# Order of the first loads and of the first projections in a four-layer transformer kernel on one Trainium2 core

## The chip, the cores and the metric

The program runs on 1 core of one Trainium2 chip. The metric is the device time of one execution in microseconds. The kernel before took 2897.74 us (median of 3 runs, 2897.18 to 2898.78). TensorE is PE below (its weight loads PEld), VectorE DVE, ScalarE ACT, GpSimd POOL, SyncE SP; a "q" behind a name (SPq) is that engine's sequencer, which also issues DMAs.

## What is computed

Two blocks of two layers each over a 512 x 1024 activation, all in float32. Each layer norms its input, projects it, mixes tokens by several kinds of attention, and runs a gated feed-forward part with a short convolution. Only the start of the first layer matters here: the norm, and the first of six column groups of its input projection.

```python
def rmsnorm(x, g):
    xf = x.astype(jnp.float32)
    y = xf * lax.rsqrt(jnp.mean(xf * xf, axis=-1, keepdims=True) + EPS)
    return (y * g.astype(jnp.float32)).astype(x.dtype)
...
def even_mixer(h, w_in, lam_params, subln_g, w_out, rel_table, lam_init):
    B, S, _ = h.shape
    qa, ka, va, qd, kd, vd = split_cols(h @ w_in, EVEN_IN_SPLIT)
```

## The kernel before

The 512 tokens are four tiles of 128 (x0 to x3, t = 0 to 3). Every float32 product is made of three products of split operands: an operand is rounded to a short float (`hi`, on ACT), and the rest is `lo = src - hi` (on DVE); `mm3` (L356 to L360) adds sl*mh, sh*ml and sh*mh into one bank. So a projection matmul needs the split activation (`hh`, `hl`, written by `split`, L390 to L393) and the split weights (`wh`, `wl`).

**Weights** come through `Stream`. `load` (L282) brings the next chunk of 512 KB into one of three raw buffers `wr` by SP's queue; `prep` (L290) makes `wh` on ACT (L300) and `wl` on DVE (L301) and loads further chunks as raw buffers come free. Four split pairs are held.

**The norm** (`pre_norm`, L410) has three stages for a tile: `sumsq` (L420: square with a running sum on ACT), `scale` (L425: `rstd` by two POOL instructions, L405 and L406, then x * rstd * gain row on DVE, L427) and `turn` (L429: eight 128 x 128 transposes on PE, L434, four to a bank, each bank split into hh and hl, half 0 holding column blocks 0 to 3 and half 1 blocks 4 to 7). The gain row is loaded to all partitions (L415). `staged` (L451) writes the stages out skewed over the tiles, and calls `fill` for finished tiles only once all four tiles are in the pipeline.

**The first projection** is "va" in `Block1.even` (L817): four weight chunks c of two column blocks each, 6 matmuls for a chunk and a tile, so 4 x 4 x 6 = 96 matmuls into four banks. `fill(t)` does chunks 0 and 1 for tile t, `vrest` (L891) chunks 2 and 3. Then "vd" and the rest of the layer follow.

**What sets the order.** A tile framework schedules the instructions of each engine itself from the order of the code and the dependencies; on an engine the resulting order is fixed and each instruction waits in turn. Loads at the start go out on SP in the order of the code in `build` (L1857 to L1864): x0, x1, two weight chunks, x2, x3; the gain row and the identity for the transposes go by ACT's queue; three small tables by POOL's.

Of the kernel before, what the change touches and what calls it, by code (L numbers as in the profile page):

```python
# [9 lines left out]
F32 = mybir.dt.float32  # L10
F32R = mybir.dt.float32r
AF = mybir.ActivationFunctionType
# [4 lines left out]
P, S, D, NT, KT = 128, 512, 1024, 4, 8  # L17
# [234 lines left out]
class Blocks:  # L252


    def __init__(self, pool, prefix, n, shape):
        self.pool, self.shape, self.free, self.tag, self.n = pool, shape, deque(f"{prefix}{i}" for i in range(n)), {}, 0
        self.prefix = prefix
# [15 lines left out]
class Stream:  # L273


    def __init__(self, k, w, plan):
        self.k, self.w, self.plan = k, w, plan
        self.loaded = self.prepped = self.lo = self.hi = 0
        self.raw, self.parts = {}, {}
        self.pool = 0  # L280

    def load(self):  # L282
        i = self.loaded
        raw = self.k.sb.tile([P, CH], F32, name=f"wr{i}", tag="wr", bufs=RAW)
        n = self.plan[i][2]
        self.k.nc.sync.dma_start(raw[:, :n], self.w[i, :, :n])
        self.raw[i] = raw
        self.loaded += 1
# [37 lines left out]
class Kernel:  # L326
# [63 lines left out]
    def split(self, hi, lo, src):  # L390

        self.nc.scalar.copy(hi, src)  # L392
        self.nc.vector.tensor_sub(lo, src, hi.bitcast(F32))  # L393
# [16 lines left out]
    def pre_norm(self, gsrc, goff, queue=None):  # L410

        nc = self.nc
        e = self.b8.get()
        grow = e[:, :D]
        (queue or nc.sync).dma_start(grow, self.row(gsrc, goff, D))  # L415
        hb = self.b8.get()
        hs = [hb[:, :D], hb[:, D:]]
        ss = {}

        def sumsq(t):  # L420
            s = self.small()
            nc.scalar.activation(e[:, D:], self.x[t], AF.Square, accum_out=s)
            ss[t] = s

        def scale(t):  # L425
            r = self.rstd(ss.pop(t), 1.0 / D)
            nc.vector.scalar_tensor_tensor(hs[t % 2], self.x[t], r, grow, op0=ALU.mult, op1=ALU.mult)  # L427

        def turn(t):  # L429
            for half in range(2):  # L430
                b = self.bank(2 * t + half)
                for j in range(4):
                    c = (4 * half + j) * P
                    nc.tensor.transpose(b[:, j * P:(j + 1) * P], hs[t % 2][:, c:c + P], self.ident)  # L434
                src = b.rearrange("p (k q) -> p k q", k=4)
                dst = (slice(None), slice(4 * half, 4 * half + 4), slice(t * P, (t + 1) * P))
                self.split(self.hh[dst], self.hl[dst], src)

        def end():
            self.b8.put(e, hb)  # L440

        def first(t):
            sumsq(t)

        def second(t):
            scale(t)

        self.junk = e[:, D:]
        return [first, second, turn], end
# [147 lines left out]
class Job:  # L597
# [15 lines left out]
    def tail(self):  # L613
        return self._tail(self)
# [127 lines left out]
class Block1:  # L742
# [69 lines left out]
        return tail  # L812

    def start(self):
        self.first = self.k.pre_norm(self.k.a["even_norm1"], 0, self.k.nc.scalar)

    def even(self):  # L817
        k, nc, a = self.k, self.k.nc, self.k.a
        stages, end = self.first
        Va, Vd = {}, {}  # L820
        parts, vb = [], {}

        def fill(t):
            if not parts:
                parts.extend(k.ws.get(*[("e", "va", c) for c in range(2)]))
            vb[t] = k.bank(2 * t)
            for c in range(2):
                k.r_tile(vb[t], parts[c], t, (2 * c, 2 * c + 1), S, start=c == 0, stop=c == 3)

        k.staged(stages, fill)  # L830
        end()
        self.vrest("e", "va", 2, vb, Va)
        vb = {t: k.bank(2 * t + 1) for t in range(NT)}
        self.vrest("e", "vd", 0, vb, Vd)
        self.lam()
        self.tables()
        nc.sync.dma_start(k.cols, a["cols"])
        at, n = COLS[2, "bg"]
        nc.vector.tensor_scalar(k.cols[:, at:at + 2 * n], k.cols[:, at:at + 2 * n], 0.5, None, op0=ALU.mult)
        store, out, tabs = {}, {}, {}  # L840

        def begin(p):
            def f(job):
                if p < 4:
                    tabs[p] = [self.table(2 * p), self.table(2 * p + 1)]
                else:
                    tabs[p] = [self.table(4 + p)] * 2
            return f

        def free_qk(p, tail):  # L850
            def f(job):
                fns = tail(job)
                first = fns[0]

                def g():
                    k.blk.put(*store.pop(p))
                    k.blk.put(tabs[p][0])
                    if p < 4:
                        k.blk.put(tabs[p][1])
                    first()  # L860
                    if p == 3:
                        k.blk.put(*Va.values())
                return [g] + fns[1:]
            return f

        def tab(p):
            return lambda hd, t, n: tabs[p][hd][:, 384 - t * P:]

        jobs = []
        for p in range(4):  # L870
            jobs.append(Job(k, Job.PAIR, self.heads64(store, p), tab(p), out, lambda p=p: p in store, begin(p),
                            free_qk(p, self.pair_tail(Va, lambda hd, p=p: (2 * p + hd) * 64, store, p, tabs, out, p))))
        for h in range(4):
            p = 4 + h
            jobs.append(DiffJob(k, self.heads64(store, p), tab(p), out, lambda p=p: p in store, begin(p),
                                free_qk(p, self.diff_tail(Vd, h, out, p))))

        def dense():
            for p in range(8):
                while p - 2 in store:  # L880
                    yield NEED
                yield from self.qk_proj("e", p, store)
            while 3 not in out:
                yield NEED
            yield from self.out_half("e", out)

        k.weave(dense(), k.attention(jobs), 800)
        k.blk.put(*Vd.values())
        return self.out_rest("e", out, 0)
# [9 lines left out]
            V[t] = k.blk.get()  # L899
            k.evac(V[t], vb[t])  # L900

    def lam(self):
        k, nc, a = self.k, self.k.nc, self.k.a
        b = k.blk.get()
        nc.sync.dma_start(b[:, :256], k.row(a["diff_lambda"], 0, 256))
        v = b[:, :256].rearrange("p (a b d) -> p a b d", a=2, b=2)
        pr = b[:, 256:384].rearrange("p (a d) -> p a d", a=2)
        s, e = k.small(2), k.small(2)
        nc.vector.tensor_mul(pr, v[:, :, 0], v[:, :, 1])
        nc.vector.tensor_reduce(s, pr, axis=mybir.AxisListType.X, op=ALU.add)  # L910
        nc.scalar.activation(e, s, AF.Exp)
        nc.vector.tensor_sub(k.neglam, e[:, 1:2], e[:, 0:1])
        nc.vector.tensor_scalar_add(k.neglam, k.neglam, -0.2)
        nc.sync.dma_start(k.subln, k.row(a["diff_subln"], 0, P))
        nc.vector.tensor_scalar(k.subln, k.subln, 0.8, None, op0=ALU.mult)
        k.blk.put(b)
# [928 lines left out]
def build(tc, a, plan):  # L1845
    nc = tc.nc
    with ExitStack() as ctx:
        sb = ctx.enter_context(tc.tile_pool(name="sb", bufs=1))
        ps = ctx.enter_context(tc.tile_pool(name="ps", bufs=1, space=PSUM))
        dram = ctx.enter_context(tc.tile_pool(name="dram", bufs=1, space=DRAM))  # L1850
        k = Kernel(tc, a, plan, sb, ps, dram)
        k.x = [k.const(f"x{t}", [P, D]) for t in range(NT)]
        xin = a["x"][0].rearrange("(t p) d -> t p d", p=P)
        k.ident = k.const("ident_sb", [P, P])
        k.cols = k.const("cols_sb", [P, a["cols"].shape[1]])
        b1 = Block1(k)
        nc.sync.dma_start(k.x[0], xin[0])  # L1857
        b1.start()
        nc.scalar.dma_start(k.ident, a["ident"])
        nc.sync.dma_start(k.x[1], xin[1])  # L1860
        k.ws.load()
        k.ws.load()
        for t in range(2, NT):
            nc.sync.dma_start(k.x[t], xin[t])  # L1864
        k.mhalf = k.const("mhalf", [P, 16])
        nc.gpsimd.memset(k.mhalf, -0.5)
        k.neglam = k.const("neglam", [P, 1])
        k.subln = k.const("subln_sb", [P, P])
        k.hh = k.const("hh", [P, KT, S], F32R)
        k.hl = k.const("hl", [P, KT, S], F32R)  # L1870
        ff = b1.even()
        ff = b1.odd(ff)
        b2 = Block2(k)
        ff = b2.mix(0, ff)
        ff = b2.mix(1, ff)
        b2.end(ff)
# [39 lines left out]
```

## Time and profile before

| | |
|---|---|
| median of the runs | 2897.74 us (2897.18 to 2898.78) |
| the profiled execution | 2899.27 us, of which the span from first to last instruction is 2897.2 us |
| PE busy | 98% of the span, 13612 matmuls |
| DVE, ACT, POOL busy | 54%, 38%, 4% |
| first slice of 40 (72 us) | PE busy 7 tenths, all later slices 8 or more |
| bytes moved | 287.18 MB, mean 99 GB/s; 297 GB/s in the first 20 us |

A busy share is an average. Where PE is busy nearly all the time, a change counts by how much earlier or later PE gets through a stretch of its fixed order, and what happens on other engines counts only where PE waits for it. So the stretch to read is the first 45 us, up to the end of the 96 matmuls of "va".

### The profile page before, as it was taken

The page shows a single profiled execution, that of the slowest core. Times are in us where ns is not written, and L with a number is a line of the kernel's source. Part 1 is how long each engine was busy: PE and PEld are TensorE (multiplying, and loading weights), DVE is VectorE, ACT ScalarE, POOL GpSimd, SP SyncE. Part 2 cuts the span into 40 slices and gives each one's busy share as a digit, 9 for nine tenths or more (in the row PEclk, how much of TensorE's full clock was granted, in tenths as well). Part 3 has the DMA queues.
Part 4 walks back from the last instruction along what each step waited for, and adds up shares of the span by engine and source line. Part 5 has one row for each costly group of instructions (what it writes and reads, how often), then busy time and mean ns, then how long its engine had stood idle before and what let it go on. Part 6 is the DMA issues. An engine that isn't in the chain of part 4 may idle for free.

```text
span 2897.2 us, 34898 instructions
## 1 busy us (share of the span) xinstructions
PE 2829.7 (98%) x13612; PEld 2313.4 (80%) x13612; DVE 1551.5 (54%) x2673; ACT 1111.5 (38%) x1928; POOL 124.8 (4%) x206
## 2 busy tenths in 40 slices
PE   7999999999999999989999999999989999999999
PEld 6778888887788888777777888888867787888887
DVE  3666544245755443466555465652685654666633
ACT  3443433224534332334433344431444434444422
POOL 1000000000000000030000010000230000100000
PEclk9999999999999999999999999999999999999999
DMA  4542323324323333212234223233222333332232
GB/s 161 151 129 78 109 95 96 109 93 141 83 88 102 96 101 106 89 62 85 77 99 124 96 98 98 96 104 105 81 70 70 99 108 100 103 101 95 95 102 73
DMA packets 93650, 287.18 MB, mean 99 GB/s; under 512 B 12544, under 2 KB 15488, under 8 KB 93486
## 3 DMA queue, kind: packets, MB, share of 16 engines
q1 hardware_dynamic: 92526, 283.18, 30.9%
q8 instruction: 107, 1.75, 0.3%
q10 hardware_dynamic: 864, 1.64, 0.2%
q14 instruction: 57, 0.47, 0.0%
q0 software_dynamic: 96, 0.14, 0.0%
HBM read 258.38 MB, written 2.15 MB: 90 GB/s over the span
## 4 chain that ended last, share of the span: by engine, by line
PE 64%; issue 25%; DVE 6%; POOL 2%; DMA 2%; ACT 1%; SPq 0%; POOLq 0%; DVEq 0%; ACTq 0%
PE b L358 19%; PE b L360 19%; PE b L359 19%; POOL s L406 1%; DMA k<-k 1%; PE b L657 1%; PE b L1532 1%; DMA wr<-in_w_dram 1%; DVE k L1472 1%; PE b L364 1%; DVE wl L301 1%; PE b L1787 1%; POOL s L405 1%; PE b L1835 0%; PE b L434 0%
## 5 line engine op out<-in xcount | busy, mean ns | idle before, releaser
L358 PE MATMUL b<-hh,wl 128*128 128x512 f32 (+1 forms) x2368 | 905.1, 383 | 1.8 <-ACT hh L392 1.0
L360 PE MATMUL b<-hh,wh 128*128 128x512 f32 (+1 forms) x2368 | 899.7, 380 | 0.0
L359 PE MATMUL b<-hl,wh 128*128 128x512 f32 (+1 forms) x2368 | 898.8, 380 | 0.0
L301 DVE TENSOR_TENSOR wl<-wr,wh 128x1024 fp32r<-128x1024 f32 (+1 forms) x407 | 495.5, 1220 | 540.1 <-ACT wh L300 538.0
L300 ACT CAST wh<-wr 128x1024 fp32r<-128x1024 f32 (+1 forms) x421 | 438.0, 1042 | 474.7 <-PE b L360 429.8
L358 PEld LDWEIGHTS b<-hh,wl 128*128 128x128 f32 x2368 | 446.3, 189 | 90.6 <-issue 9.5
L360 PEld LDWEIGHTS b<-hh,wh 128*128 128x128 f32 x2368 | 446.9, 189 | 83.3 <-issue 1.4
L359 PEld LDWEIGHTS b<-hl,wh 128*128 128x128 f32 x2368 | 447.2, 189 | 80.9 <-issue 2.0
L358 PE MATMUL b<-wh,k 128*128 128x512 f32 x900 | 352.8, 392 | 0.0
L359 PE MATMUL b<-wl,k 128*128 128x512 f32 x900 | 350.9, 390 | 0.0
L360 PE MATMUL b<-wh,k 128*128 128x512 f32 x900 | 350.4, 390 | 0.0
L358 PEld LDWEIGHTS b<-wh,k 128*128 128x128 f32 x900 | 169.1, 188 | 35.7 <-issue 0.8
L360 PEld LDWEIGHTS b<-wh,k 128*128 128x128 f32 x900 | 169.0, 188 | 35.3
L359 PEld LDWEIGHTS b<-wl,k 128*128 128x128 f32 x900 | 169.1, 188 | 34.1
L1233 ACT ACTIVATE e<-b,cols_sb 128x512 f32<-128x512 f32 x88 | 68.3, 776 | 153.7 <-PE b L360 153.7
L1234 DVE SCALAR_TENSOR_TENSOR e<-b,cols_sb,e 128x511 f32<-128x511 f32 x88 | 65.7, 746 | 104.6 <-ACT e L1233 104.4
L1223 DVE SCALAR_TENSOR_TENSOR e<-b,cols_sb,e 128x511 f32<-128x511 f32 x44 | 33.0, 750 | 159.2 <-ACT e L1222 159.2
L1222 ACT ACTIVATE e<-b,cols_sb 128x512 f32<-128x512 f32 x44 | 34.3, 778 | 178.1 <-PE b L360 178.1
L634 ACT ACTIVATE k<-k,s 128x256 f32<-128x256 f32 (+4 forms) x144 | 75.2, 523 | 58.7 <-DVE s L632 55.1
L359 PE MATMUL b<-wl,hh 128*128 128x512 f32 (+2 forms) x256 | 92.8, 363 | 0.4 <-DVE wl L301 0.4
L358 PE MATMUL b<-wh,hl 128*128 128x512 f32 (+2 forms) x256 | 93.1, 364 | 0.0
L398 DVE COPY e<-b 128x512 f32<-128x512 f32 (+1 forms) x112 | 63.1, 564 | 54.8 <-PE b L1835 24.1
(192 smaller groups left out, 3100.2 us busy)
## 6 DMA issues: line engine op xcount, KB each, us to landing
wr<-in_w_dram SPq DMA_DIRECT2D x451, 512.0 KB, 3.5
k<-k SPq DMA_DIRECT2D x186, 128.0 KB, 2.4
k<-brev SPq DMA_DIRECT2D x20, 256.0 KB, 3.8
x<-in_x_dram SPq DMA_DIRECT2D x4, 512.0 KB, 7.3
k<-in_rpb_dram SPq DMA_DIRECT2D x16, 128.0 KB, 3.1
wr<-in_w_dram SPq DMA_DIRECT2D x4, 448.0 KB, 3.3
e<-in_ffn_norm_dram SPq DMA_DIRECT2D x2, 512.0 KB, 3.6
e<-in_norm_mix_pre_dram SPq DMA_DIRECT2D x2, 512.0 KB, 4.2
```

The costliest lines, as they stand in the source:

```text
L300: nc.scalar.copy(hi[:, :n], raw[:, :n])
L301: (nc.gpsimd if self.pool > 0 else nc.vector).tensor_sub(lo[:, :n], raw[:, :n], hi[:, :n].bitcast(F32))
L358: mm(out, sl, mh, start=start, stop=False)
L359: mm(out, sh, ml, start=False, stop=False)
L360: mm(out, sh, mh, start=False, stop=stop)
L364: self.nc.tensor.matmul(out, s, m, start=i == 0, stop=i == len(pairs) - 1)
L398: self.nc.vector.tensor_copy(out, src)
L634: nc.scalar.activation(s[:, c], s[:, c], AF.Exp, bias=mx[:, i:i + 1], scale=-1.0, accum_out=sm[:, i:i + 1])
L1222: nc.scalar.activation(c, b, AF.Identity, bias=self.col(("cb",), m), scale=self.col(("cw", 2), m))
L1223: nc.vector.scalar_tensor_tensor(c[:, 1:], b[:, :S - 1], self.col(("cw", 1), m), c[:, 1:], op0=ALU.mult, op1=ALU.add)
L1233: nc.scalar.activation(y, b, AF.Identity, bias=self.col(("cb",), mm), scale=self.col(("cw", 1), mm))
L1234: nc.vector.scalar_tensor_tensor(y[:, 1:], b[:, :S - 1], self.col(("cw", 0), mm), y[:, 1:], op0=ALU.mult, op1=ALU.add)
```

## The change

- x0, the gain row and the first weight chunk are issued on SP's queue one behind the other; the identity stays on ACT's queue.
- Each later first load is tied to a stage that must have passed: a one-column POOL copy writes from that stage's output into the buffer that the load will fill, so the load waits for the copy and the copy for the stage. Chunk 1 waits for the square sum of x0, x1 for the scaled x0, x2 and x3 for the first split of tile 0 and 1, chunks 2 to 6 for the second split of tile 0, and three small loads (`diff_lambda`, `subln`, `cols`) for the last split of tile 3.
- `fill(t)` stands in the code right behind `turn(t)` instead of after the four tiles.
- ACT does a 16-column square on `mhalf` at the start, ahead of the first tile.

```diff
 class Stream:
...
+        self.passed = None
...
     def load(self):
...
+        if self.passed is not None:
+            self.k.nc.gpsimd.tensor_copy(raw[:, :1], self.passed)
         self.k.nc.sync.dma_start(raw[:, :n], self.w[i, :, :n])
...
     def start(self):
-        self.first = self.k.pre_norm(self.k.a["even_norm1"], 0, self.k.nc.scalar)
+        self.first = self.k.pre_norm(self.k.a["even_norm1"], 0)
 
     def even(self):
...
+        passed = k.const("passed", [P, 1])
+
+        def ask(t, stage):
+            nc.gpsimd.tensor_copy(k.x[t][:, :1], stage)
+            nc.sync.dma_start(k.x[t], xin[t])
...
-        k.staged(stages, fill)
+        def sumsq(t):
+            first(t)
+            if t == 0:
+                nc.gpsimd.tensor_copy(passed, k.junk[:, :1])
+                k.ws.passed = passed
+                k.ws.load()
+
+        def scale(t):
+            second(t)
+            if t == 0:
+                ask(1, k.normed[0][:, :1])
+
+        def split(j, t):
+            return k.hl[:, j, t * P:t * P + 1].bitcast(F32)
+
+        def last(t):
+            turn(t)
+            if t < 2:
+                ask(2 + t, split(0, t))
+            k.ws.passed = split(4, t) if t == 0 else None
+            fill(t)
+
+        k.staged([sumsq, scale, last])
...
-        self.lam()
+        self.lam(split(4, NT - 1))
         self.tables()
+        nc.gpsimd.tensor_copy(k.cols[:, :1], split(4, NT - 1))
         nc.sync.dma_start(k.cols, a["cols"])
...
+        k.mhalf = k.const("mhalf", [P, 16])
+        nc.gpsimd.memset(k.mhalf, -0.5)
+
+        nc.scalar.dma_start(k.ident, a["ident"])
+        nc.scalar.activation(k.small(16), k.mhalf, AF.Square)
         nc.sync.dma_start(k.x[0], xin[0])
         b1.start()
-        nc.scalar.dma_start(k.ident, a["ident"])
-        nc.sync.dma_start(k.x[1], xin[1])
         k.ws.load()
-        k.ws.load()
-        for t in range(2, NT):
-            nc.sync.dma_start(k.x[t], xin[t])
```

Line numbers from `load` on are 4 higher in the changed kernel, from `even` on more (L434 becomes L438, L358 L362, L427 L431, L301 L305, L405 L409).

**DVE at the program's start.** Names: wr, wh, wl are raw and split weights (the number is only the buffer's), x_63 to x_66 the four tiles, e_70 or e_75 the gain row, e_72 or e_77 the scaled tiles, b_ the banks of the transposes. Before, and then the change:

```order
L301 TENSOR_TENSOR wl_139<-wr_75,wh_138 128x1024
L301 TENSOR_TENSOR wl_147<-wr_77,wh_146 128x1024
L427 SCALAR_TENSOR_TENSOR e_72<-x_63,s_90,e_70 128x1024
L427 SCALAR_TENSOR_TENSOR e_72<-x_64,s_111,e_70 128x1024
L427 SCALAR_TENSOR_TENSOR e_72<-x_65,s_132,e_70 128x1024
L393 TENSOR_TENSOR hl<-b_5_96,hh 128x4x128
L393 TENSOR_TENSOR hl<-b_6_103,hh 128x4x128
```

```order
L305 TENSOR_TENSOR wl_117<-wr_78,wh_116 128x1024
L431 SCALAR_TENSOR_TENSOR e_77<-x_63,s_92,e_75 128x1024
L397 TENSOR_TENSOR hl<-b_6_100,hh 128x4x128
L305 TENSOR_TENSOR wl_127<-wr_88,wh_126 128x1024
L397 TENSOR_TENSOR hl<-b_7_107,hh 128x4x128
L431 SCALAR_TENSOR_TENSOR e_77<-x_64,s_161,e_75 128x1024
L431 SCALAR_TENSOR_TENSOR e_77<-x_65,s_197,e_75 128x1024
L397 TENSOR_TENSOR hl<-b_12_167,hh 128x4x128
L397 TENSOR_TENSOR hl<-b_13_174,hh 128x4x128
L305 TENSOR_TENSOR wl_134<-wr_120,wh_133 128x1024
L305 TENSOR_TENSOR wl_141<-wr_123,wh_140 128x1024
L397 TENSOR_TENSOR hl<-b_18_203,hh 128x4x128
```

The scaling of x0 now follows one weight subtraction, not two, and tile 0 is split before x1 is scaled; the scaling of x2 stands ahead of the split of tile 1, and two weight subtractions ahead of the split of tile 2.

**PE at the program's start.** Of the six matmuls of a chunk and a tile only the first row stands here. Before (21 transposes, then the matmuls of tile 0), and then the change:

```order
L434 MATMUL b_5_96<-ident_sb,e_72 128x128 x4
L434 MATMUL b_6_103<-ident_sb,e_72 128x128 x4
L434 MATMUL b_10_117<-ident_sb,e_72 128x128 x4
L434 MATMUL b_11_124<-ident_sb,e_72 128x128 x4
L434 MATMUL b_16_177<-ident_sb,e_72 128x128 x4
L434 MATMUL b_17_184<-ident_sb,e_72 128x128
L358 MATMUL b_15_164<-wh_138,hl 128x512
...
L358 MATMUL b_15_164<-wh_146,hl 128x512
...
L434 MATMUL b_17_184<-ident_sb,e_72 128x128 x3
```

```order
L438 MATMUL b_6_100<-ident_sb,e_77 128x128 x4
L438 MATMUL b_7_107<-ident_sb,e_77 128x128 x4
L362 MATMUL b_8_147<-wh_116,hl 128x512
...
L362 MATMUL b_8_147<-wh_126,hl 128x512
...
L438 MATMUL b_12_167<-ident_sb,e_77 128x128 x4
L438 MATMUL b_13_174<-ident_sb,e_77 128x128 x4
L438 MATMUL b_18_203<-ident_sb,e_77 128x128 x4
L438 MATMUL b_19_210<-ident_sb,e_77 128x128 x2
L362 MATMUL b_14_183<-wh_116,hl 128x512
...
L438 MATMUL b_19_210<-ident_sb,e_77 128x128 x2
L362 MATMUL b_8_147<-wh_133,hl 128x512
```

The 12 matmuls of tile 0 now stand ahead of the transposes of tile 1, and the 12 of tile 1 (b_14) behind most of the transposes of tile 2. Then come 3 matmuls of chunk 2, the 12 of tile 2, 1 more of chunk 2, and the transposes of tile 3.

**POOL behind its three table loads.** s_ are the sums and factors of the norm. Before, and then the change:

```order
L405 ISA
L405 TENSOR_SCALAR s_89<-s_87 128x1
L406 TENSOR_TENSOR s_90<-s_89,mhalf 128x1
L405 TENSOR_SCALAR s_110<-s_94 128x1
L406 TENSOR_TENSOR s_111<-s_110,mhalf 128x1
```

```order
L843 COPY passed<-e_75 128x1
L409 ISA
L409 TENSOR_SCALAR s_91<-s_85 128x1
L289 COPY wr_88<-passed 128x1
L410 TENSOR_TENSOR s_92<-s_91,mhalf 128x1
L830 COPY x_64<-e_77 128x1
L830 COPY x_65<-hl 128x1
L409 TENSOR_SCALAR s_160<-s_98 128x1
L410 TENSOR_TENSOR s_161<-s_160,mhalf 128x1
L289 COPY wr_120<-hl 128x1
L289 COPY wr_123<-hl 128x1
L289 COPY wr_130<-hl 128x1
```

The row "ISA" sets up POOL's instruction library. It now stands behind a copy that waits for the first square sum, and copies stand between the instructions of `rstd`. Behind the matmuls of "va" the order of every engine is the one before.

## Rows read from the trace of the kernel before

**Rows 1.** The page, busy time by engine: us (share of the span) xinstructions.

```profile
PE 2829.7 (98%) x13612; PEld 2313.4 (80%) x13612; DVE 1551.5 (54%) x2673; ACT 1111.5 (38%) x1928; POOL 124.8 (4%) x206
```

**Rows 2.** Timeline of PE: start us, us, engine, line, operation, [idle before <-releaser].

```profile
14.64 5.07 PE L434 MATMUL b<-ident_sb,e 128*128 128x128 f32 x21 [14.64 <-DVE e L427]
19.36 0.78 PE L358 MATMUL b<-wh,hl 128*128 128x512 f32 x1
...
42.37 0.39 PE L358 MATMUL b<-wh,hl 128*128 128x512 f32 x1
...
43.73 0.39 PE L358 MATMUL b<-wh,hl 128*128 128x512 f32 x1
```

**Rows 3.** The chain of waits in order of time, 0 to 48 us: start us, us, what.

```profile
2.12 8.94 DMA wr<-in_w_dram
...
13.31 1.29 DVE e L427
...
20.14 0.42 PE b L359
20.56 0.24 PE b L360
```

**Rows 4.** Timeline of ACT, 0 to 45 us.

```profile
6.09 1.06 ACT L422 ACTIVATE e<-x 128x1024 f32<-128x1024 f32 x1 [3.15 <-DMA x<-in_x_dram]
7.06 0.19 ACT L422 ACTIVATION_READ_ACCUMULATOR e<-x 128x1 f32 x1
...
9.81 1.04 ACT L300 CAST wh<-wr 128x1024 fp32r<-128x1024 f32 x1 [2.57 <-DMA wr<-in_w_dram]
11.09 1.04 ACT L300 CAST wh<-wr 128x1024 fp32r<-128x1024 f32 x1 [0.24 <-DMA wr<-in_w_dram]
...
15.80 0.59 ACT L392 CAST hh<-b 128x512 fp32r<-128x512 f32 x1 [0.24 <-PE b L434]
...
43.25 0.59 ACT L400 COPY k<-b 128x512 f32<-128x512 f32 x1 [2.13 <-PE b L360]
```

**Rows 5.** DMA issues in the first 1.0 us: KB each, us from issue to landing.

```profile
e<-in_even_norm_dram ACTq DMA_DIRECT2D x1, 512.0 KB, 5.6
x<-in_x_dram SPq DMA_DIRECT2D x1, 512.0 KB, 5.3
```

**Rows 6.** DMA issues from 21.9 to 22.5 us: a weight chunk with the queues empty.

```profile
wr<-in_w_dram SPq DMA_DIRECT2D x1, 512.0 KB, 3.4
```

**Rows 7.** Stretch of 1 us: engines' busy us, granted clock, DMA share, GB/s.

```profile
4.00:5.00 1.00, 0.00 (x0) 0.00 (x0) 0.00 (x0) 0.00 (x0) 0.00 (x0) 1.00 0.97 319
```

**Rows 8.** Groups of DVE by shape, 0 to 28 us: busy us, mean ns.

```profile
L427 DVE SCALAR_TENSOR_TENSOR e<-x,s,e 128x1024 f32<-128x1024 f32 x4 | 5.1, 1281 | 1.2 <-POOL s L406 1.2
L301 DVE TENSOR_TENSOR wl<-wr,wh 128x1024 fp32r<-128x1024 f32 x4 | 4.8, 1220 | 10.9 <-ACT wh L300 10.9
L393 DVE TENSOR_TENSOR hl<-b,hh 128x512 fp32r<-128x512 f32 x6 | 3.9, 683 | 0.3 <-ACT hh L392 0.3
```

**Rows 9.** Timeline of POOL, 0 to 20 us.

```profile
7.34 0.18 POOL L405 TENSOR_SCALAR s<-s 128x1 f32<-128x1 f32 x1 [4.25 <-ACT e L422]
7.60 0.57 POOL L406 TENSOR_TENSOR s<-s,mhalf 128x1 f32<-128x1 f32 x1
...
15.09 1.29 POOL L405 TENSOR_SCALAR s<-s 128x1 f32<-128x1 f32 x1
```

**Rows 10.** Line 405, 0 to 20 us: duration ns min/median/max, first and last start us.

```profile
L405 POOLq MODIFY_POOL_CONFIG  x2: 37/37/37, 3.1 to 3.1; - x2
```

**Rows 11.** PE behind a pause of 2.20 us much later: timeline, then stretches as in Rows 7.

```profile
1319.55 0.50 PE L1816 MATMUL b<-k,k 128*128 128x512 f32 x1 [2.20 <-ACT k L1819]
...
1321.56 0.63 PE L358 MATMUL b<-hh,wl 128*128 128x512 f32 x1
...
1321.00:1322.00 1.00, 1.00 (x4) 0.72 (x4) 1.00 (x3) 0.77 (x2) 0.00 (x0) 0.50 0.50 197
...
1324.00:1325.00 1.00, 1.00 (x7) 0.83 (x6) 0.14 (x1) 0.63 (x2) 0.00 (x0) 0.84 0.00 0
```

More of the change, by code (lines that the diff above doesn't have):

```diff
@@ L416, in pre_norm @@
         hb = self.b8.get()
-        hs = [hb[:, :D], hb[:, D:]]
+        hs = self.normed = [hb[:, :D], hb[:, D:]]
         ss = {}
@@ L814, in start @@
     def start(self):
-        self.first = self.k.pre_norm(self.k.a["even_norm1"], 0, self.k.nc.scalar)
+        self.first = self.k.pre_norm(self.k.a["even_norm1"], 0)
     def even(self):
         k, nc, a = self.k, self.k.nc, self.k.a
-        stages, end = self.first
+        (first, second, turn), end = self.first
         Va, Vd = {}, {}
         parts, vb = [], {}
+        xin = a["x"][0].rearrange("(t p) d -> t p d", p=P)
+        passed = k.const("passed", [P, 1])
+        def ask(t, stage):
+            nc.gpsimd.tensor_copy(k.x[t][:, :1], stage)
+            nc.sync.dma_start(k.x[t], xin[t])
         def fill(t):
@@ L900, in vrest, with lam @@
             k.evac(V[t], vb[t])
-    def lam(self):
+    def lam(self, passed):
         k, nc, a = self.k, self.k.nc, self.k.a
         b = k.blk.get()
+        nc.gpsimd.tensor_copy(b[:, :1], passed)
+        nc.gpsimd.tensor_copy(k.subln[:, :1], passed)
         nc.sync.dma_start(b[:, :256], k.row(a["diff_lambda"], 0, 256))
@@ L1856, in build @@
         b1 = Block1(k)
+        k.mhalf = k.const("mhalf", [P, 16])
+        nc.gpsimd.memset(k.mhalf, -0.5)
+        nc.scalar.dma_start(k.ident, a["ident"])
+        nc.scalar.activation(k.small(16), k.mhalf, AF.Square)
         nc.sync.dma_start(k.x[0], xin[0])
         b1.start()
-        nc.scalar.dma_start(k.ident, a["ident"])
-        nc.sync.dma_start(k.x[1], xin[1])
         k.ws.load()
-        k.ws.load()
-        for t in range(2, NT):
-            nc.sync.dma_start(k.x[t], xin[t])
-        k.mhalf = k.const("mhalf", [P, 16])
-        nc.gpsimd.memset(k.mhalf, -0.5)
         k.neglam = k.const("neglam", [P, 1])
```

## The prediction

> **What bounds the kernel now.** I read the busy shares first: PE works 98% of the span [rows 1], so outside its pauses only PE's own work counts. Then PE's timeline from the start: nothing until 14.64 us, 21 transposes until 19.36, and from there projections without a pause; two of them six places apart start 1.36 us apart, so one takes 0.227 us [rows 2]. The 96 matmuls of "va" end when ACT's last copy of a bank is let go, at 43.25 [rows 4]. The chain of waits says what the 14.64 us are: the second weight chunk lands at 11.06, is rounded and subtracted, and the scaling of x0 stands behind that on DVE although x0 has long been there [rows 3, 4]. Everything behind 43 us keeps its order on every engine. So the change is worth what it moves that 43.25, and the kernel follows by the same amount.
>
> **What there is to win at most.** If PE never paused once started, the gain would be the earlier start of the first transpose, some 4 us by the working below: 0.14%. I call a difference under 0.2% (5.8 us, about what a measurement of this kernel can tell from no change) the same.
>
> **The start, step by step.** x0 and the gain row, issued together on two queues, took 5.3 and 5.6 us [rows 5]; a chunk alone takes 3.4 [rows 6]. In one queue x0, issued at 0.74, has the engines nearly to itself: landed at 4.15 (bounds 4.1 and the old 6.0). The gain row and chunk 0 follow. Two queued chunks landed 1.3 us apart [rows 4], which gives 5.45 and 6.75; at the 319 GB/s of the early microseconds [rows 7] 512 KB need 1.65, which gives 7.45. I take 7.0 for chunk 0. Then cast 1.05, subtraction 1.22, scaling 1.28 [rows 4, 8]: 8.05, 9.3, 10.6. PE's first transpose at 10.65 instead of 14.64: **4.0 us earlier**. The norm factor of x0 is ready before: square and sum 1.25 [rows 4], three copies and two instructions of `rstd` (0.2 each for copies, like the 0.18 of a one-column instruction; 0.26 start to start and 0.57 [rows 9]), so 6.7 against the 9.3 at which DVE can use it. That is 2.6 us of cover for anything late on POOL.
>
> The hh cast began 1.16 us after the first transpose [rows 2, 4], takes 0.59, the subtraction 0.68: the first half of tile 0 is split at 13.1, and the first projection starts there instead of 19.36, **6.2 us earlier**. Chunk 1 (asked for at 6.3, landed at 9.7, split at 14.4) is in time.
>
> **What comes back.** Only 12 matmuls can run now: they end by 18.2 at the half rate that the first ones had, or by 16 at full rate. Tile 1 has just been asked for. Scaled x0 at 10.6, copy 0.2, landing 3.4, square 1.25, `rstd` 0.85, scaling 1.28: 17.65, transposes to about 19.5. Tile 2: split at 13.1, copy, 3.4, 1.25, 0.85, 1.28: 20.1. The split of tile 1 stands behind that scaling on DVE (20.1 + 0.68 = 20.8), so its 12 matmuls start at 20.9. By then the old order had done 5 of them and 21 transposes, the new one 12 and 22: of 6.2 us some 1.6 are left. This is the step on which all rests: before, all tiles were in flight at once; now a tile is requested when the one before has been worked on, and one such turn takes 7 us where PE has 2.7 us of matmuls for it.
>
> From 20.9 the supply holds. Tile 1 (2.7), two transposes (0.3), 3 of chunk 2 (0.7) reach 24.6. Tile 2's split stands behind two weight subtractions. Chunk 3, third of three copies behind `rstd` (16.35 + 0.6), lands at 21.3; its cast ends 23.05, subtraction 24.3, split 24.95: a pause of 0.4. Twelve matmuls and one: 27.9. Tile 3: copy behind the split at 20.8, landing 24.4, square behind an ACT cast 25.95, `rstd` 26.8, scaling 28.1: a pause of 0.2, 8 transposes to 29.1. Of the 96 matmuls 40 are done; 56 x 0.227 = 12.7 gives 41.8. The same point before: 43.25 less the 0.07 of the release and the 0.16 by which a matmul's record outlasts its turn, 43.0. So **-1.2 us**.
>
> **The other edits.** Ten of the copies stand in this stretch. A one-column POOL instruction took 0.18 us with DVE quiet and 1.29 beside its long instructions [rows 9]; so each copy costs 0.2 to 1.3. On the path are those for x1, x2 and x3; DVE waits when x1's runs, while a weight subtraction follows close behind the splits that release x2's and x3's. Bounds 0 and 2.2; I take 0.5, as the copy can start before the subtraction. ACT's small square at the start ends before x0 lands. The late chunks 4 to 6 are needed at 42 and asked for by 25, the three small loads are needed by idle-enough DVE before that, at about 36: nothing, under cover of 56 queued matmuls; if that cover went, each would show as a PE wait on wl. The row "ISA" appears as a configuration of POOL at 3.1 [rows 10]; the first instruction ran at 7.34, right when ACT had finished. Its cost is 0 to 4.2 us; up to 2.6 is covered, so 0 to 1.6. I take 0, since nothing was seen late. The Trainium skill has a rule against this (GPSIMD Engine Reference, 2.1 Instruction dispatch): the first call into a newly loaded kernel library pays about 6 us. The trace does not agree, 4.2 us being all the room there was; by the rule 3.3 us would reach the path and the sum would be +2.6, not -0.7.
>
> **Sum.** -1.2 + 0.5 = -0.7 us. The profiled execution was 2899.27 (span 2897.2 and 2.07 around it), which becomes 2898.6. It stood 1.5 above the median 2897.74, so the forecast for a median is **2897.0**, its own range -2 to +0.6 us: 2895.7 to 2898.3.
>
> **Rivals.**
> 1. *PE falls back to half rate* (slower). The first projections took 0.42 until 20.56, then 0.24 [rows 3]: 1.2 and 2.4 GHz, though the clock column reads 1.00 there. Much later PE paused 2.20 us, and shortly after ran at a granted 0.50 (1.2 GHz) for three stretches of 1 us in a row and part of a fourth, matmuls at 0.63 instead of 0.39 [rows 11]: about 3.4 us, 1.7 lost. The new order has such pauses between 12 and 21 us. Half rate before 20.9 costs nothing, the tiles being late anyway; it decides once it reaches the 28 matmuls after that. One such spell gives +1.0 (2898.7), two +2.7, **2900.4**. For it: the pauses; against: at half rate the early work fills most of them. The Trainium skill says the same of pauses (TensorE: Matmul & The Clock Gate, HAM oscillation): waits between short bursts send the clock back to half. These rows agree.
> 2. *POOL sets the pace* (slower). Both late copies wait a whole DVE instruction and the configuration takes the 4.2 us it may: -1.2 + 2.2 + 1.6 = +2.6, **2900.3**. For it: 13 more instructions in POOL's strict order; against: DVE is quiet at most of them. The rule of the Trainium skill quoted above (GPSIMD Engine Reference, 2.1) would also end here, at +2.6.
> 3. *The turns are shorter*, PE keeps its early start: down to -4.0, **2893.7**. It needs tile 1 split by 16, 5 us less than worked out; only a part seems open, as the landing alone takes 3.4.
> 4. *The layout.* The new constant takes 32 bytes ahead of the weight and block buffers, which so start 32 bytes later. If that changed a matmul by 1 ns, 13612 of them [rows 1] are 13.6 us: 2911 or 2884. No row shows such an effect, nor excludes it.
>
> **How the numbers follow.** Forecast 0.52, rival 1 0.18, rival 2 0.13, rival 3 0.11, rival 4 0.06. The range takes in rivals 1 to 3 with 0.6 for the spread of runs on top: 2893.7 to 2901.0. Only rival 4, and 1 and 2 together at their worst (-1.2 + 3.4 + 2.2 + 1.6 = +6.0), leave the 0.2%: slower 0.045, faster 0.035, same 0.92.
>
> **What would show it.** Right: first transpose near 10.7, first projection near 13.1, a PE wait for the scaling of x1 or x2 that ends near 20, and the last copy of "va" within 2 us of 43.25, later phases shifted alike. Rival 1: projections at 0.42 after 21. Rival 2: copies of over 1 us, or a late first `rstd`. Rival 3: no PE pause behind 13. Rival 4: means of the large matmul groups moved. It would be wrong if a phase behind 45 us changed by more than its shift.

## The result, and the profile after

The changed kernel takes 2932.12 us (median of 4 runs, 2931.64 to 2933.07) against 2898.26 for the kernel before beside it (4 runs, 2897.18 to 2898.92): ratio 1.0118, 95% interval 1.0100 to 1.0135. That is **33.9 us slower**, far outside the predicted 2893.7 to 2901.0.

The page first, as in [rows 1]: busy time by engine, us (share of the span) xinstructions, of the changed kernel (span 2930.3 us, execution 2932.41).

```profile
PE 2865.9 (98%) x13612; PEld 2312.6 (79%) x13612; DVE 1551.7 (53%) x2673; ACT 1111.9 (38%) x1929; POOL 125.2 (4%) x219
```

PE has the same 13612 matmuls and works 36.2 us longer on them (2829.7 before); DVE and ACT are within 0.5 us. PE's idle time even fell, from 67.5 to 64.4 us (span less busy). So nothing waits longer: matmuls themselves are longer. Which ones is a question for the groups of PE by shape (x count | busy us, mean ns | idle before). Of the kernel before:

```profile
L358 PE MATMUL b<-hh,wl 128*128 128x512 f32 x2112 | 833.9, 395 | 0.8 <-DVE k L1610 0.8
L360 PE MATMUL b<-hh,wh 128*128 128x512 f32 x2112 | 827.8, 392 | 0.0
L359 PE MATMUL b<-hl,wh 128*128 128x512 f32 x2112 | 826.5, 391 | 0.0
L358 PE MATMUL b<-wh,k 128*128 128x512 f32 x900 | 352.8, 392 | 0.0
...
L359 PE MATMUL b<-hl,wh 128*128 128x256 f32 x256 | 72.3, 285 | 0.0
...
L358 PE MATMUL b<-wh,hl 128*128 128x512 f32 x160 | 63.2, 396 | 0.0
```

The same groups of the changed kernel (L362 to L364 are L358 to L360):

```profile
L362 PE MATMUL b<-hh,wl 128*128 128x512 f32 x2112 | 846.1, 401 | 0.8 <-DVE k L1645 0.8
L364 PE MATMUL b<-hh,wh 128*128 128x512 f32 x2112 | 839.3, 397 | 0.0
L363 PE MATMUL b<-hl,wh 128*128 128x512 f32 x2112 | 838.5, 397 | 0.0
L362 PE MATMUL b<-wh,k 128*128 128x512 f32 x900 | 352.7, 392 | 0.0
...
L363 PE MATMUL b<-hl,wh 128*128 128x256 f32 x256 | 71.8, 283 | 0.0
...
L362 PE MATMUL b<-wh,hl 128*128 128x512 f32 x160 | 64.6, 405 | 0.5 <-DVE hl L397 0.5
```

The three groups of hh and hl with the split weights, 512 columns wide, are 12.2, 11.5 and 12.0 us longer: 35.7 of the 36.2. The matmuls against block buffers k (x900) did not change, and the 256-column ones are 2 ns shorter. It is no matter of the clock either, which is granted at 0.995 in the mean as before. The ends of matmuls are modelled in these records; the starts in PE's timeline, in a steady stretch, show the same without them. Of the changed kernel, two matmuls of one run with 30 steps between them:

```profile
299.82 0.40 PE L362 MATMUL b<-hh,wl 128*128 128x512 f32 x1
...
306.82 0.40 PE L362 MATMUL b<-hh,wl 128*128 128x512 f32 x1
```

and of the kernel before:

```profile
299.83 0.39 PE L360 MATMUL b<-hh,wh 128*128 128x512 f32 x1
...
306.63 0.39 PE L360 MATMUL b<-hh,wh 128*128 128x512 f32 x1
```

7.00 against 6.80 us for 30 steps: 0.2333 against 0.2267 us for one. None of these instructions is touched by the diff. What the diff does to them is where their operands lie.

**The start.** Timeline of PE in the changed kernel, beside [rows 2]:

```profile
11.74 1.97 PE L438 MATMUL b<-ident_sb,e 128*128 128x128 f32 x8 [11.74 <-DVE e L431]
14.26 0.79 PE L362 MATMUL b<-wh,hl 128*128 128x512 f32 x1 [0.55 <-DVE hl L397]
...
17.41 0.60 PE L363 MATMUL b<-wl,hh 128*128 128x512 f32 x1
17.83 0.40 PE L364 MATMUL b<-wh,hh 128*128 128x512 f32 x1
...
21.47 0.88 PE L438 MATMUL b<-ident_sb,e 128*128 128x128 f32 x6 [1.29 <-DVE e L431]
22.10 0.48 PE L362 MATMUL b<-wh,hl 128*128 128x512 f32 x1
...
30.67 1.09 PE L438 MATMUL b<-ident_sb,e 128*128 128x128 f32 x8 [1.57 <-DVE e L431]
```

PE starts 2.9 us earlier than before and makes the first projection 5.1 us earlier, then waits for the scaled tiles 2 and 3, 1.29 and 1.57 us. ACT's timeline, beside [rows 4], has the causes and the end:

```profile
4.89 1.06 ACT L426 ACTIVATE e<-x 128x1024 f32<-128x1024 f32 x1 [2.19 <-DMA x<-in_x_dram]
...
8.19 1.04 ACT L304 CAST wh<-wr 128x1024 fp32r<-128x1024 f32 x1 [2.14 <-DMA wr<-in_w_dram]
...
18.04 1.06 ACT L426 ACTIVATE e<-x 128x1024 f32<-128x1024 f32 x1 [1.26 <-POOL wr L289]
...
44.91 0.59 ACT L404 COPY k<-b 128x512 f32<-128x512 f32 x1 [2.21 <-PE b L364]
```

Chunk 0 is cast at 8.19. The square of x2 at 18.04 is put down to a POOL copy into a weight buffer, which it does not read; x2, issued about 14.4 and 3.5 us under way, is the likelier releaser (the record of a_same_gap, below, names the load of x for the same row). The last copy of a "va" bank is at 44.91, 1.7 us later than before.

### The profile page after: what moved, and what is told of

Its sections match the earlier page's. It is cut to its first block, busy times and chain, and to the rows that moved or that the text cites. A ratio compares the mean times of both kernels' runs of the same rounds, so it can differ in the third digit from the quotient of the medians.

```text
span 2930.3 us, 34920 instructions
## 1 busy us (share of the span) xinstructions
PE 2865.9 (98%) x13612; PEld 2312.6 (79%) x13612; DVE 1551.7 (53%) x2673; ACT 1111.9 (38%) x1929; POOL 125.2 (4%) x219
## 4 chain that ended last, share of the span: by engine, by line
PE 82%; DVE 7%; issue 5%; POOL 2%; DMA 2%; ACT 1%; SPq 0%; POOLq 0%; DVEq 0%; ACTq 0%
PE b L362 25%; PE b L364 25%; PE b L363 25%; PE b L661 1%; PE b L368 1%; POOL s L410 1%; PE b L1567 1%; DMA k<-k 1%; DVE k L1507 1%; DVE wl L305 1%; DMA wr<-in_w_dram 1%; PE b L808 1%; PE b L1822 1%; DVE e L431 1%; PE b L438 1%
## 5 line engine op out<-in xcount | busy, mean ns | idle before, releaser
L362 PE MATMUL b<-hh,wl 128*128 128x512 f32 (+1 forms) x2368 | 916.9, 388 | 1.7 <-ACT hh L396 1.0
L364 PE MATMUL b<-hh,wh 128*128 128x512 f32 (+1 forms) x2368 | 910.6, 385 | 0.0
L363 PE MATMUL b<-hl,wh 128*128 128x512 f32 (+1 forms) x2368 | 910.3, 385 | 0.0
L305 DVE TENSOR_TENSOR wl<-wr,wh 128x1024 fp32r<-128x1024 f32 (+1 forms) x407 | 495.6, 1220 | 550.2 <-ACT wh L304 548.9
L362 PEld LDWEIGHTS b<-hh,wl 128*128 128x128 f32 x2368 | 446.0, 189 | 101.0 <-issue 9.5
L364 PEld LDWEIGHTS b<-hh,wh 128*128 128x128 f32 x2368 | 446.4, 189 | 95.3 <-issue 1.4
L362 PE MATMUL b<-wh,k 128*128 128x512 f32 x900 | 352.7, 392 | 0.0
L364 PE MATMUL b<-wh,k 128*128 128x512 f32 x900 | 350.4, 390 | 0.0
L362 PEld LDWEIGHTS b<-wh,k 128*128 128x128 f32 x900 | 169.1, 188 | 35.7 <-issue 0.8
L364 PEld LDWEIGHTS b<-wh,k 128*128 128x128 f32 x900 | 169.0, 188 | 34.9
L362 PE MATMUL b<-wh,hl 128*128 128x512 f32 (+2 forms) x256 | 94.3, 369 | 0.5 <-DVE hl L397 0.5
L364 PE MATMUL b<-wh,hh 128*128 128x512 f32 (+2 forms) x256 | 92.8, 364 | 0.0
```

The source lines that it names most:

```text
L305: (nc.gpsimd if self.pool > 0 else nc.vector).tensor_sub(lo[:, :n], raw[:, :n], hi[:, :n].bitcast(F32))
L362: mm(out, sl, mh, start=start, stop=False)
L363: mm(out, sh, ml, start=False, stop=False)
L364: mm(out, sh, mh, start=False, stop=stop)
```

## The experiments

Two theories at the outset: the new constant `passed`, 32 bytes for each partition and taken behind `hh` and `hl` but ahead of the split weights and the block buffers, moves operands against each other; or the new order of loads and copies disturbs the rest. Below, "distance" is that from the start of hh to the start of wh, in bytes of a partition, as the built programs place them. Before it is 35328 (138 x 256), in the changed kernel 32800 (128 x 256 + 32). The distance from wh to k is 32768 in both. The other 2560 bytes of the difference (10 x 256) are the small buffers of the norm, which the change asks for earlier and so moves ahead of hh; a_same_gap below keeps this move and is as fast as the kernel before.

**The shift alone.** The kernel before with an unused constant at the same place, no load or order changed.

```diff
         def fill(t):
             if not parts:
+                k.const("pad", [P, 8])
```

> The kernel before with nothing changed but an unused 32-byte column ahead of wh, wl and the block buffers, so that these lie at the addresses of the changed kernel (32 bytes past a multiple of 64) and hh, hl stay on a multiple of 64. Layout theory: the difference of start address between hh, hl and wh, wl slows each of their matmuls by some 6 ns (0.227 to 0.233 us apart): 2930 to 2935 us. Rival, the new order of loads and projections or its later consequences: 2896 to 2900 us.

Measured: 2931.64 us against 2900.02 (ratio 1.0108, 1.0093 to 1.0123). Groups by shape of this kernel, from the same view:

```profile
L358 PE MATMUL b<-hh,wl 128*128 128x512 f32 x2112 | 845.4, 400 | 0.8 <-DVE k L1611 0.8
L360 PE MATMUL b<-hh,wh 128*128 128x512 f32 x2112 | 838.7, 397 | 0.0
L359 PE MATMUL b<-hl,wh 128*128 128x512 f32 x2112 | 838.0, 397 | 0.0
```

32 unused bytes alone make the whole loss. The start of this kernel is that of before (last copy 43.03).

**Is it alignment to 64 bytes?** The whole change with `passed` 64 bytes long, so that wh starts at a multiple of 64 again.

```diff
-        passed = k.const("passed", [P, 1])
+        passed = k.const("passed", [P, 16])[:, :1]
```

> The whole change, with its one-column constant made 64 bytes wide, so that wh, wl and the blocks start on a multiple of 64 like hh and hl. Layout theory: matmuls 0.227 us apart again, and what is left is the change's own effect on the start, +0.5 to +2 us: 2898 to 2901 us. Rival, order: 2930 to 2934 us.

Measured: 2930.65 us, ratio 1.0107 (1.0092 to 1.0122), groups 400, 397 and 397 ns. A miss: 64 bytes are as bad as 32.

**Position or distance?** The kernel before with the 32 bytes ahead of hh, so that all operands move together; and with 32 bytes ahead of hh and 32 ahead of wh, so that hh and hl are off by 32 and wh by 64.

```diff
# b_all32
+        k.const("pad", [P, 8])
         k.hh = k.const("hh", [P, KT, S], F32R)
# b_h32: that one, and in fill
+                k.const("pad", [P, 8])
```

> The kernel before with the unused 32-byte column ahead of hh, so that hh, hl, wh, wl and the blocks all lie 32 bytes past a multiple of 64. If the slowdown comes from the streamed and the loaded operand standing differently against 64 bytes: 2896 to 2900 us. If it comes from wh and wl lying off a multiple of 64 by themselves: 2925 to 2935 us.

> The kernel before with hh and hl 32 bytes past a multiple of 64 and wh, wl and the blocks on one: the reverse of the changed kernel. Difference theory: slow as well, 2925 to 2935 us. Theory that wh and wl must lie on a multiple of 64: 2896 to 2900 us.

Measured: b_all32 2900.55 us, ratio 1.0001 (0.9992 to 1.0010), groups 395, 391 and 391 ns; b_h32 2930.48 us, ratio 1.0108 (1.0091 to 1.0125), groups 400, 397 and 397. So it is not where the operands lie (32 bytes on for all of them change nothing) but how far hh and hl are from wh and wl.

**The change without the shift.** The whole change, with `passed` taken ahead of hh: distance 32768.

```diff
+        k.passed = k.const("passed", [P, 1])
         k.hh = k.const("hh", [P, KT, S], F32R)
...
-        passed = k.const("passed", [P, 1])
+        passed = k.passed
```

> The whole change, with its constant taken ahead of hh instead of behind hl: from hh to wh there are then 32768 bytes (a multiple of 512, like the 35328 of the kernel before), where the changed kernel has 32800. Theory that the distance from the streamed to the loaded operand must be a multiple of some power of two above 64: 0.2267 us a matmul again and only the start is left, +1 to +3 us on the kernel before run beside it. Rival, the order and its consequences: +30 to +34 us.

Measured: 2901.68 us (11 runs) against 2899.18 (15 runs), ratio 1.0005 (0.9996 to 1.0014). Groups, and the end of "va" on ACT's timeline:

```profile
L362 PE MATMUL b<-hh,wl 128*128 128x512 f32 x2112 | 833.7, 395 | 0.8 <-DVE k L1645 0.8
```

```profile
44.43 0.59 ACT L404 COPY k<-b 128x512 f32<-128x512 f32 x1 [2.13 <-PE b L364]
```

So the loads and the new order by themselves cannot be told from no change over the whole kernel, and "the same" was the forecast for them. The agreement does not go far, since in 2900 us any move of a few us is "the same"; at the start the forecast was a gain, and they lose: 44.43 against 43.25 in the kernel before and 42.38 to 42.86 in three others of this distance whose start runs as before (b_all32, b_pad256, f_only).

**Which distances?** The kernel before, with 128, 256 and 480 unused bytes ahead of wh.

```diff
+                k.const("pad", [P, 32])   # 64 and 120 in the others
```

> The kernel before with 128 unused bytes ahead of wh, wl and the blocks: distance hh to wh 128 past a multiple of 512. If the distance has to be a multiple of 128: 2896 to 2902 us, matmuls 0.2267 us apart. If of 256 or 512: 2925 to 2935 us, 0.2333 us apart.

> The same with 256 unused bytes. If the distance has to be a multiple of 256: 2896 to 2902 us; if of 512: 2925 to 2935 us.

> The same with 480 unused bytes, so the distance is 32 short of a multiple of 512 instead of 32 past one. If only being a multiple counts: 2925 to 2935 us. If the sign counts (one operand just ahead of the other): below 2910 us.

Measured, one run each: 2926.95, **2897.93** and 2929.14 us; first group 400, 395 and 400 ns (the kernel before beside them, 15 runs: 2893.88 to 2903.09). So 32, 64 and 128 bytes past a multiple of 256, and 32 short of one, are slow; exact multiples of 256, even or odd ones, are not. Below, an "odd" distance is one that is no multiple of 256.

**Which buffer against which?** Three more kernels, each the one before with a single odd buffer: wl, hl, or k (all its blocks) stands 32 bytes off; 224 more bytes behind wl or hl put the rest right again.

```diff
# b_wl32, in prep; b_k32 has only the last two of these lines, with [P, 8]
+        if i == 0:
+            self.k.const("padl", [P, 8])
         lo = self.k.sb.tile([P, CH], F32R, name=f"wl{i}", tag="wl", bufs=HB)
+        if i == 0:
+            self.k.const("padk", [P, 56])
# b_hl32
         k.hh = k.const("hh", [P, KT, S], F32R)
+        k.const("padh", [P, 8])
         k.hl = k.const("hl", [P, KT, S], F32R)
+        k.const("padw", [P, 56])
```

> The kernel before, with 32 unused bytes between the wh and the wl buffers and 224 more behind wl, so that wl alone stands 32 bytes past a multiple of 256 from hh, hl and k; wh keeps its distance to all of them to a multiple of 256. The three matmuls of a block follow one another as (hh streamed, wl loaded), (hl, wh), (hh, wh). Theory, own pair: a matmul is long when the operand it streams and the one that was loaded for it are off, so the step from L358 to L359 is 0.233 us and the other two 0.227. Rival, overlap: it is long when the weights of the next matmul, loaded while it streams, are off, so the step from L360 to L358 is 0.233 and the other two 0.227. Both give one third of the large groups (2112 x 6.5 ns = 14 us) and the 900 matmuls that stream wl against k (6 us): 2918 to 2923. A third reading, that some other part of the layout slows every matmul: all three steps 0.233, about 2930.

> The kernel before, with 32 unused bytes between hh and hl and 224 more behind hl, so that hl alone stands 32 bytes past a multiple of 256 from hh, wh, wl and k. Of the three matmuls of a block only L359 streams hl. Theory, streamed operand against the weights loaded beside it: L359 alone is long (397 ns for 391), L358 and L360 keep 395 and 392, about 2112 x 6 ns = 13 us: 2911 to 2916. Rival, the whole block: one odd buffer among the four makes the run of three take 0.700 us for 0.680 as in the kernel with wl alone off, whichever of the three the records show as long: 2926 to 2936.

> The kernel before, with 32 unused bytes between wl and the block buffers k, so that hh, hl, wh and wl keep their distances and k alone is off from wh and wl. Theory, the distance counts for every pair of a streamed and a loaded operand: the groups wh,k and wl,k (3 x 900) and k,wl and k,wh (3 x 220) get 5 to 7 ns a matmul longer (392 and 390 to about 397), the large groups of hh and hl keep 395, 392 and 391: about 3360 x 6 ns = 20 us, 2914 to 2922. Rival, only the weight buffers against hh and hl matter (another reason in those buffers): all groups as before, 2896 to 2904.

Measured: wl odd 2944.16 us against 2902.15 (ratio 1.0154, 1.0137 to 1.0171); hl odd 2922.45 and k odd 2921.90 beside 2899.64, one run each. Groups by shape, wl odd (line numbers +4):

```profile
L364 PE MATMUL b<-hh,wh 128*128 128x512 f32 x2112 | 845.8, 400 | 0.0
L363 PE MATMUL b<-hl,wh 128*128 128x512 f32 x2112 | 836.7, 396 | 0.0
L362 PE MATMUL b<-hh,wl 128*128 128x512 f32 x2112 | 833.2, 395 | 0.8 <-DVE k L1614 0.8
```

hl odd:

```profile
L358 PE MATMUL b<-hh,wl 128*128 128x512 f32 x2112 | 842.2, 399 | 0.8 <-DVE k L1610 0.8
L359 PE MATMUL b<-hl,wh 128*128 128x512 f32 x2112 | 840.2, 398 | 0.0
L360 PE MATMUL b<-hh,wh 128*128 128x512 f32 x2112 | 829.8, 393 | 0.0
```

k odd (line numbers +2):

```profile
L360 PE MATMUL b<-hh,wl 128*128 128x512 f32 x2112 | 834.5, 395 | 0.8 <-DVE k L1612 0.8
...
L360 PE MATMUL b<-wh,k 128*128 128x512 f32 x900 | 357.8, 398 | 0.0
L361 PE MATMUL b<-wl,k 128*128 128x512 f32 x900 | 356.2, 396 | 0.0
L362 PE MATMUL b<-wh,k 128*128 128x512 f32 x900 | 355.7, 396 | 0.0
```

With k odd the groups with k, and only they, are 4 to 6 ns longer, as the theory of pairs had it: the rule is not one of hh, hl and the weights. The other two forecasts missed. With wl odd the time grew by twice the forecast: 27.5 us in the three large groups and, against k, 10.9 us in the groups x900. With hl odd the 22.8 us lie between my two forecasts.

The forecasts spoke of steps, from one start to the next, and these need no modelled ends. Mean steps in ns behind each of the three matmuls of a block, from the starts in the traces (1907 to 2051 of each kind, behind 50 us and without pauses; operands as streamed, loaded):

| kernel | behind (hh, wl) | behind (hl, wh) | behind (hh, wh) | block |
|---|---|---|---|---|
| before | 227.7 | 227.2 | 227.1 | 682 |
| changed | 233.3 | 233.3 | 233.2 | 700 |
| wl odd | 228.8 | 232.5 | 238.4 | 700 |
| hl odd | 231.5 | 234.5 | 228.5 | 695 |

The records of PE and of its weight loads show which load runs beside which matmul. With wl odd:

```profile
300.64 0.40 PE L364 MATMUL b<-hh,wh 128*128 128x512 f32 x1
300.64 0.19 PEld L362 LDWEIGHTS b<-hh,wl 128*128 128x128 f32 x1
300.88 0.39 PE L362 MATMUL b<-hh,wl 128*128 128x512 f32 x1
300.88 0.19 PEld L363 LDWEIGHTS b<-hl,wh 128*128 128x128 f32 x1
```

wl is loaded while (hh, wh) streams, and that step is the longest, +11 ns, as the rival "overlap" had it; the matmul that uses wl has +1, so the theory of a matmul's own pair falls. With hl odd the longest is the step in which hl streams, +7. In both the step ahead of the longest is longer too, by 5 and 4 ns, which neither forecast had, and a block with wl alone odd takes as long as one with both wh and wl odd. So a step is long when the operand streamed in it and the one loaded beside it are at an odd distance, and the step ahead of it as well. Why the step ahead, and why 256 bytes count, stays open.

Sorting all such steps by the distance from the operand streamed to the one loaded beside it tells two more things. The kernel before already has 154 steps at 160 past a multiple of 256, beside loads of e blocks, and they take 233.7 ns against 227.5 for its other 9934. And not every odd distance costs the same: where the neighbouring steps are at an odd distance too, 32, 64, 96 and 224 past a multiple give 233.0 to 233.5, 128 gives 232.7, but 192 (64 short) only 229.1 to 229.3 (345 steps in a_pad64, 154 in the changed kernel, 154 in a_same_gap).

**One part of the change alone.** f_only: loads and layout as before, projections written behind each tile's split (the order of PE hardly moves, since the tiles come together). l_only: the tied loads in one queue, distance a multiple of 256, projections written behind the four tiles. The framework interleaves them at the start much as in the change, so l_only tells the loads from the place in the code, not from the order on PE.

```diff
# f_only: in even, loads as before
-        k.staged(stages, fill)
+        first, second, turn = stages
+
+        def last(t):
+            turn(t)
+            fill(t)
+
+        k.staged([first, second, last])
# l_only: against the whole change with passed ahead of hh
-            k.ws.passed = split(4, t) if t == 0 else None
-            fill(t)
+            k.ws.passed = split(4, 0)
-        k.staged([sumsq, scale, last])
+        k.staged([sumsq, scale, last], fill)
+        k.ws.passed = None
```

> One part of the change alone: the projections of a tile stand in the code right behind its split; loads and layout are those of before. Theory (the loads that wait for a stage make the start late, and the distance of the operands makes the rest slow): the loads all go out at once as before, so PE starts near 14.6 us and the last copy of the va banks lies where before has it, 42.4 to 43.3 us; large groups 395 and 391 ns; time within 4 us of before. Rival (the new place of the projections costs the time at the start, by half-rate matmuls and pauses between them): last copy at 44 us or later.

> The other part alone: the first loads in one queue, the later ones tied to stages, distance of the operands a multiple of 256 bytes; the projections are filled in the code behind the four tiles as before. Theory: the turns of request, landing and scaling set the pace, so PE starts near 11.8 us, waits for the scaled x1, x2 and x3 near 19, 21.5 and 30.5 us, and the last copy of the va banks lies at 44 to 45 us as in the whole change with the distance mended (44.43). Rival (the place of the projections in the code costs it): last copy at 43.3 us or earlier.

Measured, one run each: f_only 2899.10 us, PE from 14.68, last copy 42.86: the start of before. l_only 2898.91 us, last copy 44.48. Its PE timeline:

```profile
11.92 1.97 PE L438 MATMUL b<-ident_sb,e 128*128 128x128 f32 x8 [11.92 <-DVE e L431]
...
19.30 0.63 PE L364 MATMUL b<-wh,hh 128*128 128x512 f32 x1
...
21.57 1.09 PE L438 MATMUL b<-ident_sb,e 128*128 128x128 f32 x8 [0.52 <-DVE e L431]
...
30.52 1.09 PE L438 MATMUL b<-ident_sb,e 128*128 128x128 f32 x8 [1.48 <-DVE e L431]
```

The tied loads bring the late start with them. Here all of the first twelve projections ran at half rate, to 19.7 us instead of the 17.8 of the changed kernel, and tile 2 was still waited for until the same 21.5: PE's rate is not what sets this stretch, the tiles' arrival is.

**Can the queue be had without the ties?** All first loads in one queue in the order of need, none tied, projections behind each split, layout of before.

```diff
-        self.first = self.k.pre_norm(self.k.a["even_norm1"], 0, self.k.nc.scalar)
+        self.first = self.k.pre_norm(self.k.a["even_norm1"], 0)
...
+        nc.scalar.dma_start(k.ident, a["ident"])
         nc.sync.dma_start(k.x[0], xin[0])
         b1.start()
-        nc.scalar.dma_start(k.ident, a["ident"])
-        nc.sync.dma_start(k.x[1], xin[1])
         k.ws.load()
+        nc.sync.dma_start(k.x[1], xin[1])
         k.ws.load()
```

> All first loads in one queue in the order of need (x0, gain row, chunk 0, x1, chunk 1, x2, x3), none tied to a stage, projections behind each tile's split, layout of before. Theory: x0 and chunk 0 come as early as in the change (PE starts at 11.5 to 12.5 us instead of 14.6) and the later tiles do not wait for a turn, so the last copy of the va banks lies at 39.5 to 42 us instead of 42.4 to 43.3, large groups 395 and 391 ns, ratio 0.9985 to 1.000. Rival (one queue is slower whatever is tied to it, since transfers stand behind one another): last copy at 43 us or later, ratio 1.000 or above.

Measured: 2899.65 us (11 runs) against 2900.67 (15 runs), ratio 0.9996 (0.9987 to 1.0005). PE starts at 12.16, and its waits behind 16 us are gone; the end of "va" on ACT:

```profile
41.44 0.59 ACT L400 COPY k<-b 128x512 f32<-128x512 f32 x1 [2.13 <-PE b L360]
```

That is 0.9 to 1.8 us earlier than the starts named above and 3.0 earlier than the change with its distance mended. It is the best start of all these, and still not to be told from no change in 2900 us.

## Why the prediction was wrong

**The step that failed** is "Everything behind 43 us keeps its order on every engine. So the change is worth what it moves that 43.25, and the kernel follows by the same amount." The order did stay; the durations did not. Rival 4 named the cause (the constant's 32 bytes ahead of the weight and block buffers) and its test (means of the large groups), though as a later start and not as a distance, and "No row shows such an effect, nor excludes it" was turned into a chance of 0.06 and kept out of the range. Its example of a size was off too: not 1 ns on 13612 matmuls (13.6 us) but 5 to 6 ns on the 6336 of the three large groups (35.7 us), no change on the 2700 against k, whose distance to the weights had not moved, and 2 ns the other way on the 256-column ones. An unpriced effect that would touch every matmul deserved a place in the range; a kernel with nothing but the shift moved would have priced it.

**The start** was forecast at -0.7 us, -2 to +0.6. Without the shift it came out at +1.2 in these records (44.43 against 43.25), and +1.6 to +2.1 against the three other starts of the old kind: outside that range and the other way. By its own steps:
- Turns set the pace: right. PE waits for the scaled x2 until 21.5 (forecast 20.1) and for x3, and queue_free, which takes the ties away, loses those waits.
- "I take 7.0 for chunk 0": mis-sized. x0 was squared at 4.89 (landing forecast 4.15), the chunk, issued third, cast at 8.19, past the slow bound of 7.45. The first transpose came at 11.74 instead of 10.65, the first projection at 14.26 instead of 13.1, tile 1's at 22.10 instead of 20.9: the same 1.1 to 1.2 us all along.
- "Tile 3: ... landing 24.4 ... a pause of 0.2": mis-sized. x3 was issued at 22.29 and took 4.8 us, not the 3.4 of a chunk alone [rows 6]. DMA issues of the changed kernel in 22.2 to 22.5 us (KB each, us to landing), and the stretches around it (busy us of PE, PEld, DVE, ACT, POOL, granted clock, DMA share, GB/s):

```profile
x<-in_x_dram SPq DMA_DIRECT2D x1, 512.0 KB, 4.8
```

```profile
21.00:22.00 1.00, 0.53 (x5) 0.53 (x6) 1.00 (x3) 0.59 (x1) 0.00 (x0) 1.00 1.07 410
...
26.00:27.00 1.00, 1.00 (x6) 0.82 (x5) 0.69 (x1) 0.00 (x0) 0.00 (x0) 1.00 0.91 258
```

  The DMA share was 1.07 and 0.91 in these two stretches and 0.68 to 1.08 between them. Three weight chunks had been asked for from 17.86 to 19.43, ahead of x3, and two more from 24.02 on; that sharing the DMA engines with them held x3 up is likely, but was not tested. The pause was 1.57 us instead of 0.2, and 1.39 in a_same_gap:

```profile
30.48 1.09 PE L438 MATMUL b<-ident_sb,e 128*128 128x128 f32 x8 [1.39 <-DVE e L431]
```

  The 1.2 of chunk 0 and the 1.2 by which this pause was too short make the miss: the last copy stood in the sum at 43.25 - 1.2 = 42.05 without the 0.5 for the POOL copies, and a_same_gap has it at 44.43.
- "I take 0.5" for the POOL copies: too much. Timeline of POOL, beside [rows 9]:

```profile
6.11 0.18 POOL L843 COPY passed<-e 128x1 f32<-128x1 f32 x1 [3.01 <-ACT e L426]
6.40 0.18 POOL L409 TENSOR_SCALAR s<-s 128x1 f32<-128x1 f32 x1
...
17.65 1.43 POOL L289 COPY wr<-hl 128x1 f32<-128x1 f32 x3
```

  The three copies on the path (at 11.75, 14.26 and 22.08) took 0.18 each, and the -1.2 had 0.2 for each already, so nothing came on top; the slow ones, 1.43 for three beside DVE's scaling, were weight chunks. The library's set-up row, which stands between the first two rows here, cost nothing to be seen: 0.11 us lie between them. The price that the Trainium skill names for a first call (GPSIMD Engine Reference, 2.1) is not met here either. So rival 2 did not come.
- Rival 1 (half rate after 21 us) did not come: steps of 0.23 from 22.4 on. Nor did rival 3: PE paused ahead of 21.47 and 30.67. Part of what it had in mind shows in queue_free, which has other loads.

## What to carry to other kernels

A change that takes a new buffer also moves every buffer behind it: compare the operands' distances before and after, and put small constants ahead of all matmul operands, or pad so that operands that are streamed and loaded together keep a multiple of 256 bytes. When PE's busy time changes with the same matmuls, read its groups by shape before any wait. At the start of a kernel a queue in the order of need gives the early start; tying each load to the work on the one before gives it back, because a landing of 3.5 to 4.8 us and the work on a tile are longer than the matmuls that one tile offers.

## What the runs showed of the hardware

- A 512-column matmul of these split floats starts every 0.2267 us when the streamed and the loaded operands lie a multiple of 256 bytes apart, and every 0.2333 us at 32 past one, also when all of them are moved by 32; 64, 128 and 32 short are as slow or nearly so (0.2324 to 0.2334), 64 short only 0.229. 256-column ones rather gain (285 against 283 ns, and 121.5 against 120.0 from start to start behind (hl, wh)).
- The extra time need not fall on the matmul that uses the odd operand: with wl odd the step behind that one had 1 ns more, the step in which wl was loaded 11 ns and the one ahead of that 5.
- At the start matmuls ran at half rate for some 6 us behind the first transpose in the changed kernel and 8 us in l_only, at a granted clock that the rows show as 1.00 throughout.
